# Merge gates as seven block products at the end of the first network, values of two groups there too, and square sums and scalings on ScalarE

## Chip, core and metric

The kernel runs on one core of one Trainium2 chip. The time is device microseconds of one execution; 2530.77 us is the median of 3 runs of the kernel before (2530.6 to 2532.81). A profile is one further execution, with its own time. PE is TensorE, DVE VectorE, ACT ScalarE, POOL GpSimd, SP the queue from which most transfers are issued.

## What is computed

One decoder layer on x of 1024 tokens x 1024 channels, all in float32:

```
x = x + 1/2 * SwiGLU_1(RMSNorm(x))
h = RMSNorm(x);  p = h @ w_in       # columns: q, k, v of 3 attention groups; q, k, v, beta,
                                    # decay and gate of 8 delta heads; merge gates g_a, g_b
A = dilated windowed attention, 3 groups x 4 heads of 64, softmax over the groups
B = gated delta rule, 8 heads of 128 (conv of 4 + silu, unit q and k, chunks), RMSNorm * silu(gate)
y = (sig(g_a) * (A @ w_branch_a) + sig(g_b) * (B @ w_branch_b)) @ w_out;   x = x + y
x = x + 1/2 * SwiGLU_2(RMSNorm(x));  out = RMSNorm(x)
```

g_a and g_b are 1024 x 1024 each: eight blocks of 128 columns of w_in for each, 16 in all.

## The kernel before

**Matmuls.** A float32 product is made of three float32r products: each operand v is split into H (v rounded, by an ACT copy) and L = v - H (by DVE), and xH wH + xL wH + xH wL is summed in PSUM. `ff_split` (L208 on, rows L216 and L217) splits a weight tile of 128x512, `split_to` (L166, L167) an activation. `proj` (L152 on, row L161) makes one 128-column block for one half of the 512 tokens with 8 k x 3 matmuls of 512 columns. Activations h are held transposed as `hH`, `hL`.

**First network** (`ff_hidden`, `ff_pair`, `ff_products`): the hidden blocks are made in pairs of columns. h (channels x tokens) and each weight pair are cut in 2x2 blocks, and seven block products (Winograd's form) stand in for eight: sums of blocks of h are made once (`ff_blocks`: T1, T2, T3, and a changed B12), the sums of the weight blocks per pair, and the products are accumulated or added in four PSUM banks (`QUAD_BANKS`) in the order `STEPS`. The first pairs use the order `FIRST`, which starts with products that need no sums (row L404). The down projection (`Down`, row L588) is a block form too. Its closing steps make h for the mixer (`make_h`), and then `First` multiplies h with the value columns of group 0 and the beta and decay columns (row L805), four token blocks before the last turns of h and four after, and stores them.

**Mixer** (`mixer`): three attention groups, each with its values (`values`: groups 1 and 2 as 16 token blocks x 24 matmuls of 256 columns, L701, evicted by ACT, stored and read back in another order), two pairs of heads with rotary q and k, and blocks of scores (L870), exp and products with V (L894). Then 8 delta heads. Per head: `gdn_keys` projects k and q, convolves them (L963 copy out of PSUM, L971 and L973 the four taps), transposes them (L983), squares and sums them per token (`ssq_tokens`: ACT square of 128x512 at L986, DVE reduction at L987), makes the decay matrix Dm (L1012 to L1015), and N and A as products of k and q with k (L1139) times a per-token factor and Dm (L1142, one DVE operation per chunk of 128). `gdn_inverse` sends blocks of N through DRAM, solves 32 rows on DVE (L1044 to L1050), sends them back, transposes (L1060) and merges the blocks with small matmuls (L1078 to L1100). `gdn_values` makes vb (L1164, L1165), `gdn_gate` the head's gate, `gdn_scan` runs over eight chunks one after the other (L1195 to L1219), squares and sums the output (L1226, L1227), scales it and transposes it (L1236).

**Merge gates** (`gate_tile`): one block of 128 columns is 2 x 24 matmuls into bank "mm", an ACT copy (L950) and a store for each half. `FILL` says how many are put where: two with the last attention pair, eight with the heads, the remaining six with the last head, together with `branch_a`. `merge_out` reads them back and multiplies.

**Order.** The program is traced once, `arrange` plans an order of the instructions for each engine from costs of its own (`Program.cost`) by the longest path to the end, and the kernel is built again with that order. It keeps the rings of tiles and of PSUM banks in the order of the program: "mm" has 2 banks, "ka" 9 tiles (k, q, kd, N and A of a head take five), "xp" 2, "vb", "g" and "Tm" 1. Tiles of a pool that is opened later wait for those of a closed one at the same place.

Of the kernel before, what the change touches and what calls it, by code (L numbers as in the profile page):

```python
# [8 lines left out]
F32 = mybir.dt.float32  # L9
# [275 lines left out]
    return res  # L285


def ff_blocks(C):


    nc = C.nc
    T1, T2, T3 = [[] for _ in range(3)]
    for i, T in ((2, T2), (1, T1), (3, T3)):
        for q in range(2):
            h, l = [C.fx.tile([P, 2, 512], F32R, name=f"t{i}{n}", tag="big", bufs=12) for n in "HL"]
            T += [(h[:, k], l[:, k]) for k in range(2)]
# [4 lines left out]
    keep = []

    def sums(ks):
        for k in ks:
            r = []
            for kk, ts in ((k, lo), (k, hi), (4 + k, lo), (4 + k, hi)):
                v = ff_e(C)
                nc.vector.tensor_tensor(out=v, in0=hH[:, kk, ts].bitcast(F32), in1=hL[:, kk, ts].bitcast(F32), op=ALU.add)
# [375 lines left out]
    return t[rows, (b - 1 if prev else b) * P:(b + 1) * P]  # L684


def values(C, I, w_in, g):

    nc = C.nc
    n = 256  # L690
    W = []
    with band(C, "bulk"):
        for k0 in (0, 4):
            halves = load_w(C, (lambda r: r[:, :4 * n].rearrange("p (k n) -> p k n", n=n),
                                cols(w_in, C_VA + g * 256, 256)[:, k0:k0 + 4, :]))
            W += [[v[:, i * n:i * n + n] for v in pair] for pair in halves for i in range(2)]
        for b in range(NT):
            ps = psum(C, "mm")
            for k in range(KT):
                for i, (h, w) in enumerate(((C.hH, 0), (C.hH, 1), (C.hL, 0))):  # L700
                    nc.tensor.matmul(ps[:, :n], h[:, k, b * P:b * P + P], W[k][w],  # L701
                                     start=k == 0 and i == 0, stop=k == KT - 1 and i == 2)
            v = C.at.tile([P, 256], F32, name="vs", tag="vs", bufs=2)
            nc.scalar.copy(v, ps[:, :256])
            nc.sync.dma_start(C.vd[g - 1][b * P:b * P + P, :], v)
# [77 lines left out]
class First:  # L783
# [193 lines left out]
def ssq_tokens(C, src, kd, out):  # L977

    nc = C.nc
    for q in range(2):  # L980
        ps = psum(C, "tA")
        for c in range(4):
            nc.tensor.transpose(ps[:, c * P:c * P + P], src[:, q * 4 + c, :], C.ident)  # L983
        v = ps.rearrange("p (c t) -> p c t", t=P)
        sq = C.gd.tile([P, 4, P], F32, name="sq", tag="sq", bufs=1)
        nc.scalar.activation(sq, v, AF.Square)  # L986
        nc.vector.tensor_reduce(out=out[:, q * 4:q * 4 + 4], in_=sq, axis=AX.X, op=ALU.add)  # L987
# [120 lines left out]
def gdn_keys(C, w_in, h, Dm):  # L1108
# [4 lines left out]
    with band(C, f"h{h}"):  # L1113
# [11 lines left out]
        ns = cl[:, 4]  # L1125
# [8 lines left out]
        for src, dst, sc in ((X.k, X.N, ns), (X.q, X.A, s)):  # L1134
            for q in range(2):
                ps = psum(C, "tA")
                for i in range(4):
                    c = q * 4 + i
                    nc.tensor.matmul(ps[:, i * P:i * P + P], X.k[:, c, :], src[:, c, :], start=True, stop=True)  # L1139
                for i in range(4):  # L1140
                    c = q * 4 + i
                    nc.vector.scalar_tensor_tensor(dst[:, c, :], ps[:, i * P:i * P + P], sc[:, c:c + 1], Dm[:, c, :],  # L1142
                                                   op0=ALU.mult, op1=ALU.mult)
# [10 lines left out]
def gdn_values(C, w_in, X):  # L1154
    nc = C.nc
    h = X.h
    with band(C, f"h{h}"):
# [3 lines left out]
        for q in range(2):  # L1161
            ps = psum(C, "tA")
            for c in range(4):
                nc.tensor.transpose(ps[:, c * P:c * P + P], vT[:, q * 4 + c, :], C.ident)  # L1164
            nc.vector.tensor_tensor(out=X.vb[:, q * 4:q * 4 + 4, :], in0=ps.rearrange("p (c t) -> p c t", t=P),  # L1165
                                    in1=X.nk[:, q * 4:q * 4 + 4].unsqueeze(2).to_broadcast([P, 4, P]), op=ALU.mult)
# [13 lines left out]
def gdn_scan(C, X):  # L1180
# [6 lines left out]
    with band(C, f"h{h}"):  # L1187
# [33 lines left out]
                S = Sn  # L1221

        so2 = C.gd.tile([P, 2, NT], F32, name="so2", tag="so2", bufs=2)
        for q in range(2):
            sq = C.gd.tile([P, 4, P], F32, name="sq", tag="sq", bufs=1)
            nc.scalar.activation(sq, o[:, q * 4:q * 4 + 4, :], AF.Square)  # L1226
# [683 lines left out]
```

## Times and profile before

| | |
|---|---|
| median of 3 runs | 2530.77 us |
| profiled execution, its own time | 2533.24 us |
| its span, first to last instruction | 2531.4 us |
| mean granted TensorE clock | 0.995 |
| network 1 up to its down projection | 0 to about 450 us |
| down projection and first values | about 450 to 703 us |
| attention | about 703 to 993 us |
| delta heads | about 980 to 1705 us |
| merge, norm and start of network 2 | about 1705 to 1931 us |
| network 2 | about 1931 to 2531 us |

Matmuls are pipelined, so that the busy time of one overlaps the next; the time of one in a stream is best read as a window's length over its count. A row of the groups names line, engine, operation, output<-inputs, shapes and count, then busy time, mean ns of one, and the engine's idle time before them with what ended it. A row of the table of windows gives each engine's busy time and count, the granted PE clock, the DMA share and GB/s. A row of a timeline or of the chain of waits gives start and length in us, then the engine and what it did.

### The profile page before, as it was taken

To read this page: it belongs to the slowest core of one execution; us is meant where nothing else is said; L and a number is where in the kernel's file an instruction comes from. 1 tells how busy PE (TensorE), PEld (TensorE's weight loads), DVE (VectorE), ACT (ScalarE), POOL (GpSimd) and SP (SyncE) were. 2 spreads that over 40 slices of the span, in tenths; PEclk is the share of its full clock that TensorE was granted. 3 is DMA by queue.
4 is the path that set the end of the run, shared out by engine and by line. 5 is a ranking of instruction groups with operands and counts; after the bars stand their busy time and mean duration, and the time that the engine had idled before them with its cause. 6 is when DMAs were issued, how large, how long until landed. Compare 5 with 4: busy or idle time off the path is not lost.

```text
span 2531.4 us, 34786 instructions
## 1 busy us (share of the span) xinstructions
PE 2488.5 (98%) x12739; PEld 2071.9 (82%) x12739; DVE 1766.7 (70%) x4035; ACT 983.8 (39%) x1881; POOL 26.5 (1%) x36
## 2 busy tenths in 40 slices
PE   7999999999999999999999999999999999999998
PEld 7888888888888888778777888888888888888886
DVE  7866666768734464878887888455768666667589
ACT  4432322444523346333454335254443332323444
POOL 0000000000000000000000000000000000000000
PEclk9999999999999999999999999999999999999999
DMA  4233224746343322222222223357532223238443
GB/s 163 84 109 117 92 104 175 269 125 205 122 124 94 100 78 64 61 53 55 78 65 64 55 75 84 105 200 286 199 126 83 100 92 121 90 118 305 137 163 133
DMA packets 259547, 308.39 MB, mean 122 GB/s; under 512 B 41680, under 2 KB 175024, under 8 KB 259376
## 3 DMA queue, kind: packets, MB, share of 16 engines
q1 hardware_dynamic: 257072, 299.88, 35.8%
q10 hardware_dynamic: 2304, 6.29, 1.1%
q8 instruction: 100, 1.64, 0.3%
q14 instruction: 71, 0.58, 0.1%
HBM read 221.01 MB, written 78.81 MB: 118 GB/s over the span
## 4 chain that ended last, share of the span: by engine, by line
PE 84%; DVE 11%; DMA 2%; ACT 1%; issue 1%; SPq 0%; DVEq 0%; ACTq 0%
PE mm L161 19%; PE tC L404 13%; PE mm L404 9%; PE tM L404 8%; PE mm L588 4%; PE tC L588 4%; PE tM L588 3%; PE tA L588 3%; PE tA L161 3%; PE mm L701 2%; PE mm L274 2%; PE tC L274 2%; DVE ka L973 2%; PE mm L1409 2%; PE tC L1409 1%; DVE fL L217 1%
## 5 line engine op out<-in xcount | busy, mean ns | idle before, releaser
L216 ACT CAST fH<-fraw 128x512 fp32r<-128x512 f32 x482 | 289.6, 620 | 603.4 <-PE tC L404 258.5
L217 DVE TENSOR_TENSOR fL<-fraw,fH 128x512 fp32r<-128x512 f32 x482 | 319.0, 685 | 161.5 <-ACT fH L216 147.0
L161 PE MATMUL mm<-hH,fH 128*128 128x512 f32 x896 | 360.3, 404 | 2.5 <-ACT xp L832 2.4
L161 PE MATMUL mm<-hL,fH 128*128 128x512 f32 x896 | 356.8, 399 | 0.0
L161 PE MATMUL mm<-hH,fL 128*128 128x512 f32 x896 | 353.9, 400 | 0.0
L161 PEld LDWEIGHTS mm<-hH,fH 128*128 128x128 f32 x896 | 170.1, 190 | 34.8 <-ACT xp L832 2.9
L161 PEld LDWEIGHTS mm<-hH,fL 128*128 128x128 f32 x896 | 169.6, 189 | 33.9 <-issue 1.0
L161 PEld LDWEIGHTS mm<-hL,fH 128*128 128x128 f32 x896 | 169.9, 190 | 30.5 <-issue 0.3
L404 PE MATMUL mm<-hH,fH 128*128 128x512 f32 x320 | 124.6, 389 | 0.0
L404 PE MATMUL mm<-hH,fL 128*128 128x512 f32 x320 | 123.7, 389 | 0.0
L404 PE MATMUL mm<-hL,fH 128*128 128x512 f32 x320 | 122.5, 389 | 0.0
L581 DVE TENSOR_TENSOR hid<-hid,fH 128x512 fp32r<-128x512 f32 x149 | 101.1, 684 | 10.1 <-ACT fH L580 10.1
L973 DVE SCALAR_TENSOR_TENSOR ka<-xp,cw,ka 128x512 f32<-128x512 f32 x96 | 74.9, 791 | 38.9 <-ACT ka L971 38.3
L580 ACT CAST fH<-hid 128x512 fp32r<-128x512 f32 x149 | 91.8, 616 | 14.6 <-PE tC L588 5.0
L216 ACT CAST fH<-hH 128x512 fp32r<-128x512 f32 x68 | 42.2, 622 | 84.7 <-PE tC L588 32.8
L431 DVE TENSOR_TENSOR e<-tC,e 128x512 f32<-128x512 f32 x40 | 27.3, 687 | 66.5 <-PE tC L404 66.5
L404 PEld LDWEIGHTS mm<-hH,fH 128*128 128x128 f32 x320 | 60.1, 188 | 12.7 <-ACT e L408 0.3
L404 PEld LDWEIGHTS mm<-hH,fL 128*128 128x128 f32 x320 | 60.1, 188 | 12.5
L588 PE MATMUL mm<-fH,hid 128*128 128x512 f32 x186 | 70.3, 389 | 0.0
L588 PE MATMUL tC<-fH,hid 128*128 128x512 f32 x186 | 70.3, 389 | 0.0
L404 PEld LDWEIGHTS mm<-hL,fH 128*128 128x128 f32 x320 | 60.1, 188 | 12.5
L351 DVE TENSOR_TENSOR s<-fraw 128x512 f32<-128x512 f32 x40 | 27.5, 687 | 54.0 <-DMA fraw<-in_ffn_w_gate_dram 53.4
(401 smaller groups left out, 6157.1 us busy)
## 6 DMA issues: line engine op xcount, KB each, us to landing
fraw<-in_w_in_dram SPq DMA_DIRECT2D x66, 512.0 KB, 3.8
fraw<-in_ffn_w_gate_dram SPq DMA_DIRECT2D x22, 1024.0 KB, 5.2
fraw<-in_ffn_w_up_dram SPq DMA_DIRECT2D x22, 1024.0 KB, 7.3
hL<-in_ffn_w_down_dram SPq DMA_DIRECT2D x8, 1024.0 KB, 6.6
fraw<-in_ffn_w_down_dram SPq DMA_DIRECT2D x8, 1024.0 KB, 5.9
fraw<-in_w_branch_b_dram SPq DMA_DIRECT2D x8, 1024.0 KB, 5.0
fraw<-in_w_out_dram SPq DMA_DIRECT2D x8, 1024.0 KB, 5.6
vb<-xp ACTq DMA_DIRECT2D x48, 128.0 KB, 2.4
```

What stands on the lines that cost most here:

```text
L161: nc.tensor.matmul(ps, w, x, start=k == 0 and i == 0, stop=k == kt - 1 and i == 2)
L216: nc.scalar.copy(h, src)
L217: nc.vector.tensor_tensor(out=l, in0=src, in1=h.bitcast(F32), op=ALU.subtract)
L274: nc.tensor.matmul(ps[:, n0:n0 + n], w, x[:, k, c], start=k == 0 and i == 0, stop=k == KT - 1 and i == 2)
L351: tt(out=s3[i], in0=a11, in1=a21, op=ALU.subtract)
L404: nc.tensor.matmul(ps, w, x, start=opens and k == 0 and q == 0, stop=k == 3 and q == 2, skip_group_check=True)
L580: C.nc.scalar.copy(h, v.bitcast(F32))
L581: C.nc.vector.tensor_tensor(out=v, in0=v.bitcast(F32), in1=h.bitcast(F32), op=ALU.subtract)
L588: self.C.nc.tensor.matmul(ps, x[:, m], w, start=p == 0 and i == 0, stop=p == NPAIR - 1 and i == 2)
L701: nc.tensor.matmul(ps[:, :n], h[:, k, b * P:b * P + P], W[k][w], start=k == 0 and i == 0, stop=k == KT - 1 and i == 2)
L973: nc.vector.scalar_tensor_tensor(o, x, w, o, op0=ALU.mult, op1=ALU.add)
L1409: nc.tensor.matmul(ps, mx[:, c], W[k][w], start=i == 0, stop=i == len(seq) - 1)
```

## The change

Fourteen of the sixteen gate blocks are made at the end of the first network, in seven pairs, with the seven block products; the last two stay with the last head. The block sums of h are made once more there, with the changed B12 in tiles of its own (`apart`), so that h stays as it is. The value products of groups 1 and 2 move there, between the first values and the pairs; their evicted tiles share the ring "s3" of 3 tiles, as those of the first values now do. In the heads, ACT sums the squares as it makes them, one chunk of 128 at a time, and scales Dm and vb per chunk; N and A are then made four chunks at a time. The planner adds 1000 ns to the expected end of each transfer.

```diff
-def ff_blocks(C):
+def ff_blocks(C, apart=False):
...
+    T4 = B12
+    if apart:
+        h, l = [C.fx.tile([P, 4, 512], F32R, name=n, tag=n, bufs=1) for n in ("vH", "vL")]
+        T4 = [(h[:, k], l[:, k]) for k in range(4)]
...
-            split_to(C, *B12[k], v)
+            split_to(C, *T4[k], v)
...
+def value_blocks(C, w_in, g):
...
+    for b in range(NT):
+        ps = psum(C, "tM")
...
+        v = ff_e(C, "vs", tag="s3")
+        nc.scalar.copy(v[:, :n], ps[:, :n])
+        nc.sync.dma_start(C.vd[g - 1][b * P:b * P + P, :], v[:, :n])
...
+GATES = [(C_GA + f * P, 0, f) for f in range(8)] + [(C_GB + f * P, 1, f) for f in range(8)]
+APART = 14
+def gate_pair(C, B, w_in, i, steps):
+    raw = ff_raw(C, cols(w_in, GATES[i][0], 256), 256)
...
+    def prepare(n):
+        if n == 6:
+            left[7] = ff_e(C, "s3", tag="s3").rearrange("p (k n) -> p k n", n=P)
+            tt(out=left[7], in0=a11, in1=a21, op=ALU.subtract)
+            tt(out=a21, in0=a21, in1=a22, op=ALU.add)
+            tt(out=a11, in0=a21, in1=a11, op=ALU.subtract)
+        elif n == 3:
+            tt(out=a12, in0=a12, in1=a11, op=ALU.subtract)
+        return ff_split(C, {1: a11, 6: a11, 5: a21, 2: a12, 4: a22, 3: a12, 7: left.get(7)}[n])
...
+    def run(chosen):
+        for n, b, opens in chosen:
...
+            for k in range(4):
+                xH, xL = B[n][k]
+                h, l = [v[:, k * P:k * P + P] for v in (H, L)]
+                for q, (x, w) in enumerate(((xH, h), (xL, h), (xH, l))):
+                    nc.tensor.matmul(ps, w, x, start=opens and k == 0 and q == 0, stop=k == 3 and q == 2,
+                                     skip_group_check=True)
...
+def gates_apart(C, w_in, between):
+    B, sums, last = ff_blocks(C, True)
+    sums(range(4))
+    between()
+    last()
+    for i in range(0, APART, 2):
+        steps = FIRST if i < 4 else STEPS
+        gate_pair(C, B, w_in, i, steps)(steps)
...
 def ssq_tokens(C, src, kd, out):
-        sq = C.gd.tile([P, 4, P], F32, name="sq", tag="sq", bufs=1)
-        nc.scalar.activation(sq, v, AF.Square)
-        nc.vector.tensor_reduce(out=out[:, q * 4:q * 4 + 4], in_=sq, axis=AX.X, op=ALU.add)
+        for c in range(4):
+            sq = C.gd.tile([P, P], F32, name="sq", tag="sq", bufs=2)
+            nc.scalar.activation(sq, v[:, c, :], AF.Square, accum_out=out[:, q * 4 + c:q * 4 + c + 1])
...
 def gdn_keys(C, w_in, h, Dm):
-        nc.vector.tensor_scalar(ns, s, -1.0, None, op0=ALU.mult)
+        for c in range(NT):
+            nc.scalar.activation(Dm[:, c, :], Dm[:, c, :], AF.Copy, scale=s[:, c:c + 1])
...
-                for i in range(4):
-                    c = q * 4 + i
-                    nc.vector.scalar_tensor_tensor(dst[:, c, :], ps[:, i * P:i * P + P], sc[:, c:c + 1], Dm[:, c, :],
-                                                   op0=ALU.mult, op1=ALU.mult)
+                nc.vector.scalar_tensor_tensor(dst[:, q * 4:q * 4 + 4, :], ps.rearrange("p (c t) -> p c t", t=P), sign,
+                                               Dm[:, q * 4:q * 4 + 4, :], op0=ALU.mult, op1=ALU.mult)
...
 def gdn_values(C, w_in, X):
-            nc.vector.tensor_tensor(out=X.vb[:, q * 4:q * 4 + 4, :], in0=ps.rearrange("p (c t) -> p c t", t=P),
-                                    in1=X.nk[:, q * 4:q * 4 + 4].unsqueeze(2).to_broadcast([P, 4, P]), op=ALU.mult)
+            for c in range(q * 4, q * 4 + 4):
+                nc.scalar.activation(X.vb[:, c, :], ps[:, (c - q * 4) * P:(c - q * 4) * P + P], AF.Copy, scale=X.nk[:, c:c + 1])
...
 def gdn_scan(C, X):
-        for q in range(2):
-            sq = C.gd.tile([P, 4, P], F32, name="sq", tag="sq", bufs=1)
-            nc.scalar.activation(sq, o[:, q * 4:q * 4 + 4, :], AF.Square)
-            nc.vector.tensor_reduce(out=so2[:, 0, q * 4:q * 4 + 4], in_=sq, axis=AX.X, op=ALU.add)
+        for c in range(NT):
+            sq = C.gd.tile([P, P], F32, name="sq", tag="sq", bufs=2)
+            nc.scalar.activation(sq, o[:, c, :], AF.Square, accum_out=so2[:, 0, c:c + 1])
...
-FILL = ((0, 0, 0, 0, 0, 2), (1, 1, 1, 1, 1, 1, 2))
+FILL = ((0, 0, 0, 0, 0, 0), (0, 0, 0, 0, 0, 0, 0))
...
-            first.blocks(range(4, NT))
+            def between():
+                first.blocks(range(4, NT))
+                for g in (1, 2):
+                    value_blocks(C, I["w_in"], g)
+            gates_apart(C, I["w_in"], between)
...
+MARGIN = 1000
...
             wire = end - tail
+            end += MARGIN
```

More of the change, by code (lines that the diff above doesn't have):

```diff
@@ L318, in sums @@
             keep.append(r21)
+    T4 = B12
+    if apart:
+        h, l = [C.fx.tile([P, 4, 512], F32R, name=n, tag=n, bufs=1) for n in ("vH", "vL")]
+        T4 = [(h[:, k], l[:, k]) for k in range(4)]
     def last():
         for k, v in enumerate(keep):
-            split_to(C, *B12[k], v)
-    return {1: B11, 2: B21, 3: B22, 4: B12, 5: T1, 6: T2, 7: T3}, sums, last
+            split_to(C, *T4[k], v)
+    return {1: B11, 2: B21, 3: B22, 4: T4, 5: T1, 6: T2, 7: T3}, sums, last
 FIRST = ((1, 0, True), (2, 0, False), (3, 3, True), (6, 1, True), (5, 2, True), (7, 1, False), (4, 1, False))
@@ L684, in seq_tokens @@
     return t[rows, (b - 1 if prev else b) * P:(b + 1) * P]
-def values(C, I, w_in, g):
+def value_blocks(C, w_in, g):
     nc = C.nc
@@ L691, in values @@
     W = []
-    with band(C, "bulk"):
[L693 to L705, printed above, removed]
+    for k0 in (0, 4):
+        halves = load_w(C, (lambda r: r[:, :4 * n].rearrange("p (k n) -> p k n", n=n),
+                            cols(w_in, C_VA + g * 256, 256)[:, k0:k0 + 4, :]))
+        W += [[v[:, i * n:i * n + n] for v in pair] for pair in halves for i in range(2)]
+    for b in range(NT):
+        ps = psum(C, "tM")
+        for k in range(KT):
+            for i, (h, w) in enumerate(((C.hH, 0), (C.hH, 1), (C.hL, 0))):
+                nc.tensor.matmul(ps[:, :n], h[:, k, b * P:b * P + P], W[k][w],
+                                 start=k == 0 and i == 0, stop=k == KT - 1 and i == 2)
+        v = ff_e(C, "vs", tag="s3")
+        nc.scalar.copy(v[:, :n], ps[:, :n])
+        nc.sync.dma_start(C.vd[g - 1][b * P:b * P + P, :], v[:, :n])
+def values(C, I, w_in, g):
+    nc = C.nc
+    with band(C, "bulk"):
         V = [None] * NT
@@ L821, in first_values, with keep @@
     return V
+GATES = [(C_GA + f * P, 0, f) for f in range(8)] + [(C_GB + f * P, 1, f) for f in range(8)]
+APART = 14
+def gate_pair(C, B, w_in, i, steps):
+    nc = C.nc
+    tt = nc.vector.tensor_tensor
+    raw = ff_raw(C, cols(w_in, GATES[i][0], 256), 256)
+    a11, a12, a21, a22 = [raw[:, q * 4:q * 4 + 4, m * P:m * P + P] for m in (0, 1) for q in (0, 1)]
+    early = steps is FIRST
+    banks = [None] * 4
+    left = {}
+    out = [(C.sgad, C.sgbd)[GATES[i + j][1]][GATES[i + j][2]] for j in (0, 1)]
+    def prepare(n):
[7 more added lines that the diff above has]
+        return ff_split(C, {1: a11, 6: a11, 5: a21, 2: a12, 4: a22, 3: a12, 7: left.get(7)}[n])
+    def keep(j, a, v):
+        nc.sync.dma_start(out[j][:, a * 512:a * 512 + 512], v)
+    weights = {}
+    for n in (1, 2, 6, 3, 5, 7, 4) if early else [n for n, _, _ in steps]:
+        weights[n] = prepare(n)
+    def run(chosen):
+        for n, b, opens in chosen:
+            if opens:
+                banks[b] = psum(C, QUAD_BANKS[b])
+            ps = banks[b]
+            H, L = weights[n]
+            for k in range(4):
[4 more added lines that the diff above has]
+                                     skip_group_check=True)
+            if n == 1:
+                run.p1 = ff_e(C)
+                nc.scalar.copy(run.p1, ps)
+            elif n == 6:
+                run.u2 = ff_e(C)
+                tt(out=run.u2, in0=ps, in1=run.p1, op=ALU.add)
+                if early:
+                    tt(out=run.u2, in0=banks[3], in1=run.u2, op=ALU.add)
+            elif n == 7:
+                u3 = ff_e(C)
+                tt(out=u3, in0=ps, in1=run.p1, op=ALU.add)
+                tt(out=u3, in0=banks[2], in1=u3, op=ALU.add)
+                keep(1, 1, u3)
+            elif n == 2:
+                c = ff_e(C)
+                nc.scalar.copy(c, ps)
+                keep(0, 0, c)
+            elif n == 4:
+                tt(out=run.p1, in0=ps, in1=run.p1, op=ALU.add)
+                keep(1, 0, run.p1)
+            elif n == (5 if early else 3):
+                tt(out=run.u2, in0=ps, in1=run.u2, op=ALU.add)
+                keep(0, 1, run.u2)
+    return run
@@ L1130, in gdn_keys @@
         nc.vector.tensor_scalar(X.so, rs[:, 8:16], float(P) ** -0.5, None, op0=ALU.mult)
-        nc.vector.tensor_scalar(ns, s, -1.0, None, op0=ALU.mult)
+        for c in range(NT):
+            nc.scalar.activation(Dm[:, c, :], Dm[:, c, :], AF.Copy, scale=s[:, c:c + 1])
         X.N, X.A = t4c(C, "ka"), t4c(C, "ka")
-        for src, dst, sc in ((X.k, X.N, ns), (X.q, X.A, s)):
+        for src, dst, sign in ((X.k, X.N, -1.0), (X.q, X.A, 1.0)):
             for q in range(2):
@@ L1309, in mixer @@
         C.bands[f"h{h}"] = base + 100000 + 20000 * h
-    gates = [(C_GA + f * P, C.sgad[f]) for f in range(8)] + [(C_GB + f * P, C.sgbd[f]) for f in range(8)]
+    gates = [(c, (C.sgad, C.sgbd)[i][f]) for c, i, f in GATES[APART:]]
     def fill(n):
```

3 lines of the change are left out of this document (1 added, 2 removed).

## The prediction

> **What bounds the kernel now.** I read the page's first lines, then the table of windows by stage, then the groups by form, and windows, chain and timeline of single stretches.
>
> ```profile
> span 2531.4 us, 34786 instructions
> PE 2488.5 (98%) x12739; PEld 2071.9 (82%) x12739; DVE 1766.7 (70%) x4035; ACT 983.8 (39%) x1881; POOL 26.5 (1%) x36
> PE 84%; DVE 11%; DMA 2%; ACT 1%; issue 1%; SPq 0%; DVEq 0%; ACTq 0%
> ```
>
> ```profile
> core 0: us, PE busy (x) PEld busy (x) DVE busy (x) ACT busy (x) POOL busy (x), PEclk, DMA share, GB/s
> 655.00:707.00 52.00, 52.00 (x348) 48.09 (x347) 30.11 (x83) 21.44 (x43) 0.00 (x0) 1.00 0.36 116
> 707.00:950.00 243.00, 240.55 (x1462) 205.01 (x1461) 121.39 (x301) 83.42 (x243) 1.92 (x2) 0.99 0.36 100
> 950.00:1075.00 125.00, 123.92 (x704) 100.82 (x705) 84.90 (x268) 62.93 (x135) 5.30 (x6) 1.00 0.22 61
> 1075.00:1705.00 630.00, 616.63 (x3689) 509.39 (x3688) 477.69 (x1444) 263.61 (x505) 19.06 (x24) 0.99 0.28 83
> 1935.00:2310.00 375.00, 375.00 (x1654) 310.07 (x1654) 250.99 (x407) 113.39 (x200) 0.00 (x0) 1.00 0.32 115
> ```
>
> The last row is the gate and up part of the second network, which works in the same seven-product form as the new gates: PE never pauses, and one 512-column matmul takes 375.00 / 1654 = 0.2267 us (the longer means of the groups below overlap). DVE is at 67% and ACT at 30% there. The mixer is different: from 1075 to 1705 PE loses 630.00 - 616.63 = 13.4 us, and DVE is at 76%. So PE sets the time nearly everywhere, work taken from PE is time as long as PE stays fed, and the place to look for losses is the mixer, where several chains of small steps are covered by projections. The gates are part of that cover.
>
> The profiled execution took 2533.24 us (span 2531.4), against a median of 2530.77 us; I work out differences on its rows and apply them to the median.
>
> **Gates as seven products.** One gate block is 2 halves x 8 k x 3 = 48 matmuls. Fourteen blocks are 672. Seven pairs of 7 products x 4 k x 3 = 84 are 588. That is 84 matmuls fewer, 84 x 0.2267 = 19.0 us. This is the only PE work that the change removes, and it is certain.
>
> What feeds the pairs:
>
> ```profile
> L217 DVE TENSOR_TENSOR fL<-fraw,fH 128x512 fp32r<-128x512 f32 x482 | 319.0, 685 | 161.5 <-ACT fH L216 147.0 <-PE tM L404 6.8 <-DMA U<-in_rope_dram 5.7
> L216 ACT CAST fH<-fraw 128x512 fp32r<-128x512 f32 x482 | 289.6, 620 | 603.4 <-PE tC L404 258.5 <-PE mm L161 81.8 <-DVE fraw L353 52.0
> L308 DVE TENSOR_TENSOR e<-hH,hL 128x512 f32<-128x512 f32 x32 | 20.2, 682 | 0.1
> 707.00:950.00 243.00, 48.67 (x384) 47.17 (x384) 0.99 0.36 100
> ```
>
> The last row is the window table for the value line L701 alone. A pair needs 3 sums, 7 splits and 5 evictions on DVE, 15 x 0.685 = 10.3 us, and 9 ACT operations, 9 x 0.62 = 5.6 us, beside 84 x 0.2267 = 19.0 us of PE. That is 54% of DVE and 29% of ACT, less than in the row 1935:2310 where PE doesn't pause: cost 0. Should feeding fail it would show at most at the first pair, whose 10 sums and splits are 7 us; that is the upper end. Its four stores and one load leave SP's queue in the mixer for this stretch, as the values' 16 stores and 4 loads do; PE waits for none of them there, since loads run two tiles ahead.
>
> The block sums of h are new: 4 x 11 + 4 = 48 DVE operations, 48 x 0.682 = 32.7 us, with 16 ACT splits, 9.9 us. Eight splits of the value weights come before, 8 x 0.685 = 5.5 us. The cover is the 384 value matmuls, 48.7 us, and four blocks of the first values: 38 us under about 60 us. Also, the first two pairs begin with products 1, 2 and 3, which need no sum. Cost 0; without the cover, up to 38 us.
>
> **Values moved.** The same 384 matmuls run earlier; their 48.7 us vanish from the attention stage and appear before it. Cost 0 as long as attention stays bound by PE: with 243 - 49 = 194 us left, DVE's 121 us are 63%. The evicted tile now has 3 buffers instead of 13 (first values) or 2: a block lasts 24 x 0.12 = 2.9 us, so three buffers are 8.7 us for a copy and a store. Nothing is queued behind it but the next copy.
>
> **Square sums and scalings by ACT.**
>
> ```profile
> L987 DVE TENSOR_REDUCE gssq<-sq 128x4 f32<-128x512 f32 x32 | 21.7, 679 | 4.4 <-ACT sq L986 4.1
> L986 ACT ACTIVATE sq<-tA 128x512 f32<-128x512 f32 x32 | 19.0, 594 | 9.6 <-DVE gssq L987 6.7 <-PE tA L983 1.3 <-PE tM L1100 1.1
> L1226 ACT ACTIVATE sq<-vb 128x512 f32<-128x512 f32 x16 | 10.1, 630 | 28.1 <-DVE vb L1219 28.1
> L1142 DVE SCALAR_TENSOR_TENSOR ka<-tA,cl,Dm 128x128 f32<-128x128 f32 x128 | 37.9, 343 | 0.4 <-issue 0.2
> L1165 DVE TENSOR_TENSOR vb<-tA,cl x16: 652/684/701, 1045.0 to 1619.1; 128x512 f32<-128x512 f32 x16
> L973 DVE SCALAR_TENSOR_TENSOR ka<-xp,cw,ka 128x512 f32<-128x512 f32 x96 | 74.9, 791 | 38.9 <-ACT ka L971 38.3
> L1201 ACT ACTIVATE qs<-tC,ex 128x128 f32<-128x128 f32 x56 | 20.5, 366 | 79.1 <-PE tC L1199 78.9
> L1205 ACT COPY v<-tC 128x128 f32<-128x128 f32 x64 | 16.9, 264 | 47.4 <-PE tC L1203 47.3
> L880 ACT ACTIVATION_READ_ACCUMULATOR s<-s,nm 128x1 f32 x96 | 18.0, 188 | 0.0
> ```
>
> DVE loses per head 6 reductions (4.1 us), 2 scalings of vb (1.4 us), and 16 small multiplies (37.9 / 8 = 4.7 us) that become 4 wide ones (4 x 0.79 = 3.2 us): 7.0 us. ACT gains per head 24 squares with a sum read out. No row has one alone; between a copy of that size (0.264) and a scaled one (0.366), plus the read-out of 0.188, it is 0.45 to 0.55 us, so 10.8 to 13.3 us. I take 10.8, since a square takes no scale from memory. Six wide squares go (4 x 0.594 + 2 x 0.630 = 3.6 us). The 16 scalings of Dm and vb are 16 x 0.366 = 5.9 us. Net ACT +13.1 us per head.
>
> One head's period, with the gates that go:
>
> ```profile
> 1237.00:1317.00 80.00, 78.41 (x485) 64.62 (x484) 66.99 (x202) 35.47 (x66) 3.32 (x4) 1.00 0.24 65
> 1237.00:1317.00 80.00, 62.41 (x241) 42.77 (x240) 1.00 0.24 65
> 993.00:1078.00 85.00, 83.36 (x482) 67.37 (x481) 69.36 (x196) 41.50 (x66) 4.71 (x5) 1.00 0.22 57
> 993.00:1078.00 85.00, 1.76 (x3) 1.00 0.22 57
> 1573.00:1705.00 132.00, 131.76 (x725) 109.22 (x724) 72.13 (x198) 51.57 (x103) 0.00 (x0) 1.00 0.44 146
> 1573.00:1705.00 132.00, 6.99 (x12) 1.00 0.44 146
> ```
>
> Of each two rows the first is all work, the second the projections (L161) or the gates' evictions alone. In 1237:1317 there are 241 projection matmuls, five blocks of 48: k, q, v, the head's gate and one merge gate. Without the merge gate 80 - 10.9 = 69.1 us of PE are left. DVE has 67.0 - 7.0 - 1.4 (the gate's splits) = 58.6 us, 85% of that, where it was 84%. ACT has 35.5 + 13.1 - 2.4 = 46.2 us, 67%. So the three engines shrink together, and I expect the period to follow PE with a little less ease: +0.5 us for each of seven heads, +3 us in all; between -5 (less DVE ahead of PE's small matmuls than now) and +25 (the rival below).
>
> The start of the heads (993 to 1078) is the stretch with least to spare. Three evictions are one and a half gates, 16.3 us of PE, so about 69 us of PE stay. DVE's 69.4 us lose the reductions, small multiplies and splits of nearly two heads, about 12 us, and much of the stretch is a chain over DVE. I take 73 us for it, a loss of 4 us; the ends are 0 and 16.3 us (nothing else moves up).
>
> The end of the heads (1573 to 1705) held twelve evictions, six gates; two stay. 132 - 4 x 10.9 = 88.4 us of PE are left for the last head's chain (two rows of DVE's timeline, then four of the chain of waits):
>
> ```profile
> 1577.40 0.17 DVE L1044 TENSOR_TENSOR fsP<-fsT,Tm 128x16 f32<-128x16 f32 x1
> 1608.54 1.24 DVE L1060 STREAM_TRANSPOSE Tm<-U 128x1024 f32<-128x1024 f32 x1
> ```
>
> ```profile
> 1648.68 0.62 PE tM L1078 x32
> 1657.66 0.60 PE tM L1100 x8
> 1660.54 0.22 PE tC L1203 x2
> 1702.31 0.87 PE tC L1236 x8
> ```
>
> From 1577.4 the inverse takes 32.4 us to 1609.8; then its merge waits 39 us for its turn on PE; merge, scan and closing transposes take 1703.2 - 1648.7 = 54.5 us. Without the wait this is 87 us from 1577.4, 91 us from 1573, against 88.4 us of PE: a loss of 2 us, between 0 and 10.
>
> The planner's margin makes it expect each transfer 1 us later. It adds no wait, but can reorder everything; transfers hold 2% of the chain of waits, so little hangs on when they are expected. I take 0, between -3 and +4.
>
> Sum: -19.0 + 3 + 4 + 2 = -10 us, from 2533.24 to 2523 for the profiled execution, from 2530.77 to **2521 us** for the median.
>
> **The rivals.**
>
> *The heads become a chain (slower).* Keys of head h+2 reuse tiles that the scan of head h frees:
>
> ```profile
> 1345.87 0.29 DVE L1219 TENSOR_TENSOR vb<-tC,qs 128x128 f32<-128x128 f32 x1 [1.31 <-PE tC L1215]
> 1346.73 0.57 ACT L963 COPY xp<-mm 128x512 f32<-128x512 f32 x1
> 1348.09 0.75 DVE L973 SCALAR_TENSOR_TENSOR ka<-xp,cw,ka 128x512 f32<-128x512 f32 x1
> ```
>
> The scan's last output at 1345.9 is followed at once by the next-but-one head's convolution. This loop spans two periods. It decides once it takes over 2 x 69.1 = 138 us, and the new ACT work in it (squares before the inverse, scalings of Dm) lengthens it by some 7 us. Today it lasts two periods, 2 x 80 = 160 us. If the two merge gates inside are all that leaves it, it is 160 - 21.8 + 7 = 145 us, 72.7 per period, and costs 7 x 3.6 = 25 us; with the 6 us of start and end, 2531 - 19 + 25 + 6 = 2543 us. For it speaks that it restarts without slack; against it, that in the last head waiting alone was 39 us, so the loop holds much that only waits for PE. Chance 0.15.
>
> *The saving is eaten at the edges (no change).* Start and end at their far ends cost 16 + 10 = 26 us; with a third of that regained by projections pulled forward, 17 us stay: 2531 - 19 + 17 = 2529 us. Chance 0.18.
>
> *PE pauses halve its clock (slower).*
>
> ```profile
> 1376.00:1380.00 4.00, 2.39 (x25) 2.00 (x23) 3.81 (x8) 2.80 (x6) 0.00 (x0) 0.76 0.01 4
> 1380.00:1384.00 4.00, 4.00 (x14) 3.33 (x13) 3.65 (x6) 2.26 (x5) 0.00 (x0) 0.50 0.17 66
> ```
>
> After 4 us in which PE worked 2.39, the next four ran at clock 0.50, 14 matmuls: about 2 us lost. If each of eight heads brings two such stretches more, 16 x 2 = 32 us go: 2531 - 19 + 32 = 2544 us. Chance 0.04, since the rows have few now. The Trainium skill ("TensorE: Matmul & The Clock Gate", "Part 1: The HAM clock gate (the "warmup" mystery)") speaks against taking cover from PE: after an idle window of about 3.4 us the clock is halved until PE has been busy for one. The trace agrees with the halving; that the whole window must be idle it doesn't show, since a stretch with PE busy for 2.39 of 4 us was enough.
>
> *All of it is kept.* Fewer switches and no loss at the edges: 2530.8 - 19 = 2512 us or some less. Chance 0.12. That the products are not fewer I rule out by the count.
>
> **How the numbers follow.** My forecast, 2514 to 2525.7, has the remaining 0.51. About 5 us (0.2%) is what a measurement here can tell from no change. Faster by more: 0.51 + 0.12 = 0.63. Within: 0.18. Slower: 0.15 + 0.04 = 0.19. The range goes from 2508 (all kept and 3 us of reordering) to 2541, which leaves out about half of the slower cases.
>
> **What would show it.** In the profile after: 84 matmuls fewer; a stretch of some 133 us before the mixer with PE at 100% and about 0.2267 us per matmul; heads about 70 us apart instead of 81; DVE near 85% and ACT near 67% there; PE's idle time in the mixer up by some 10 us. The forecast is wrong if heads follow each other at over 72 us, if PE pauses during the gate pairs, or if the granted clock drops in more than a few stretches.

## The result and the profile after

The change takes 2495.73 us (median of 4 runs, 2495.34 to 2496.77) against 2531.79 us before: a ratio of 0.9858 (95% interval 0.9843 to 0.9872), 36 us less. I had forecast 2521 us, and 2508 as the lowest. The direction was right; the gain is nearly twice what the count of products gives.

The page after, its span, busy line and chain by engine:

```profile
span 2495.0 us, 35187 instructions
PE 2457.7 (99%) x12655; PEld 2045.7 (82%) x12655; DVE 1787.9 (72%) x4001; ACT 1052.4 (42%) x2364; POOL 25.2 (1%) x36
PE 87%; DVE 7%; DMA 2%; ACT 2%; issue 1%; SPq 0%; ACTq 0%; DVEq 0%
```

PE has 12739 - 12655 = 84 matmuls fewer, as counted. For the rest, I cut both kernels at the same events: the first rotary copy out of PSUM, and the last closing transposes of the last head. First before, then after (there with the first network's end, and cut again at the last attention block and the first scan step); columns as in the prediction.

```profile
702.70:1703.20 1000.50, 983.61 (x5861) 817.33 (x5860) 682.19 (x2010) 409.27 (x882) 26.28 (x32) 0.99 0.30 85
```

```profile
695.00:741.00 46.00, 46.00 (x379) 45.78 (x378) 26.01 (x43) 14.00 (x30) 0.00 (x0) 1.00 0.13 44
741.00:885.20 144.20, 143.53 (x634) 118.28 (x632) 73.18 (x116) 39.17 (x71) 0.00 (x0) 1.00 0.32 104
885.20:1666.40 781.20, 770.49 (x4792) 633.13 (x4791) 595.70 (x1802) 421.94 (x1257) 24.95 (x32) 1.00 0.30 85
```

```profile
885.20:1107.30 222.10, 219.27 (x1249) 177.76 (x1248) 132.89 (x371) 93.03 (x288) 1.91 (x2) 1.00 0.38 103
1107.30:1185.70 78.40, 75.90 (x462) 62.32 (x461) 63.95 (x170) 47.94 (x143) 4.22 (x6) 1.00 0.22 56
1185.70:1666.40 480.70, 475.31 (x3084) 393.05 (x3083) 398.86 (x1263) 280.96 (x828) 18.82 (x24) 1.00 0.28 81
```

The mixer went from 1000.5 to 781.2 us. What left it by count is 672 x 0.2267 + 48.7 = 201.0 us, so it got 18.3 us shorter than that. The new stage ahead of it lasts 885.2 - 702.7 = 182.5 us, where 588 x 0.2267 + 48.7 = 182.0 was to be expected: the seven products and the values run at PE's pace from the start. After the mixer both kernels take the same, 2531.4 - 1703.2 = 828.2 and 2495.0 - 1666.4 = 828.6 us. So the question is the 18 us in the mixer. PE's idle time there fell from 1000.50 - 983.61 = 16.9 to 781.20 - 770.49 = 10.7 us, where I had expected it to rise. The rest is busy time: it fell by 213.1 us, 12 more than the 201.0 counted, and part of that is the granted clock, 0.99 before and 1.00 after.

### The profile page after: what moved, and what is told of

Its sections match the earlier page's. It is cut to its first block, busy times and chain, and to the rows that moved or that the text cites. A ratio compares the mean times of both kernels' runs of the same rounds, so it can differ in the third digit from the quotient of the medians.

```text
span 2495.0 us, 35187 instructions
## 1 busy us (share of the span) xinstructions
PE 2457.7 (99%) x12655; PEld 2045.7 (82%) x12655; DVE 1787.9 (72%) x4001; ACT 1052.4 (42%) x2364; POOL 25.2 (1%) x36
## 4 chain that ended last, share of the span: by engine, by line
PE 87%; DVE 7%; DMA 2%; ACT 2%; issue 1%; SPq 0%; ACTq 0%; DVEq 0%
PE mm L161 15%; PE tC L409 13%; PE mm L409 9%; PE tM L409 8%; PE mm L593 4%; PE tC L593 4%; PE tM L593 4%; PE tA L593 4%; PE tA L161 3%; PE tC L876 2%; PE tM L705 2%; PE mm L274 2%; PE tC L274 2%; PE mm L876 2%; PE mm L1498 2%; PE tC L1498 2%
## 5 line engine op out<-in xcount | busy, mean ns | idle before, releaser
L216 ACT CAST fH<-fraw 128x512 fp32r<-128x512 f32 x496 | 298.2, 621 | 634.2 <-PE tC L409 243.0
L217 DVE TENSOR_TENSOR fL<-fraw,fH 128x512 fp32r<-128x512 f32 x496 | 329.3, 687 | 108.5 <-ACT fH L216 90.3
L161 PE MATMUL mm<-hH,fH 128*128 128x512 f32 x672 | 272.2, 406 | 2.5 <-ACT xp L924 2.1
L161 PE MATMUL mm<-hL,fH 128*128 128x512 f32 x672 | 268.3, 400 | 0.0
L161 PE MATMUL mm<-hH,fL 128*128 128x512 f32 x672 | 263.1, 399 | 0.0
L161 PEld LDWEIGHTS mm<-hH,fH 128*128 128x128 f32 x672 | 126.9, 189 | 29.2 <-ACT xp L924 4.5
L161 PEld LDWEIGHTS mm<-hH,fL 128*128 128x128 f32 x672 | 126.8, 189 | 23.5 <-issue 0.3
L161 PEld LDWEIGHTS mm<-hL,fH 128*128 128x128 f32 x672 | 126.9, 189 | 21.2
L409 PE MATMUL mm<-hH,fH 128*128 128x512 f32 x320 | 124.5, 389 | 0.0
L409 PE MATMUL mm<-hH,fL 128*128 128x512 f32 x320 | 123.3, 389 | 0.0
L409 PE MATMUL mm<-hL,fH 128*128 128x512 f32 x320 | 122.5, 389 | 0.0
L409 PEld LDWEIGHTS mm<-hH,fL 128*128 128x128 f32 x320 | 60.1, 188 | 12.5
L409 PEld LDWEIGHTS mm<-hL,fH 128*128 128x128 f32 x320 | 60.1, 188 | 12.5
L409 PEld LDWEIGHTS mm<-hH,fH 128*128 128x128 f32 x320 | 60.0, 188 | 12.5
L216 ACT CAST fH<-hL 128x512 fp32r<-128x512 f32 x56 | 34.9, 623 | 71.4 <-PE tC L593 40.5
```

The costliest lines, as they stand in the source:

```text
L161: nc.tensor.matmul(ps, w, x, start=k == 0 and i == 0, stop=k == kt - 1 and i == 2)
L216: nc.scalar.copy(h, src)
L217: nc.vector.tensor_tensor(out=l, in0=src, in1=h.bitcast(F32), op=ALU.subtract)
L409: nc.tensor.matmul(ps, w, x, start=opens and k == 0 and q == 0, stop=k == 3 and q == 2, skip_group_check=True)
```

## The experiments

The change has three parts that can be undone alone: **place** (gates as products, values, and their new place), **ACT** (squares and scalings), and the planner's **margin**. Six kernels have every mix of them.

**Margin alone**, the kernel before with:

```diff
+MARGIN = 1000
...
             wire = end - tail
+            end += MARGIN
```

> The kernel before with the planner's margin of 1000 ns alone. The change took 36 us where the product count gives 19, so 17 us are to be explained. Theory M (the margin keeps planned work from standing behind transfers): 2531 - 17 = 2514 us. Theory D (relief of DVE by ACT) and theory L (the gates' and values' place): 2531 us, within 4 us.

2520.43 us, ratio 0.9953 (0.9939 to 0.9968): 12 us less. Of the three theories this speaks for the margin, though its 17 us aren't reached; two lines of the planner, which I had priced at 0, bring a third of the result on the old kernel.

**ACT alone**, the kernel before with the four edits of `ssq_tokens`, `gdn_keys`, `gdn_values` and `gdn_scan`:

```diff
-        nc.scalar.activation(sq, v, AF.Square)
-        nc.vector.tensor_reduce(out=out[:, q * 4:q * 4 + 4], in_=sq, axis=AX.X, op=ALU.add)
+        for c in range(4):
+            sq = C.gd.tile([P, P], F32, name="sq", tag="sq", bufs=2)
+            nc.scalar.activation(sq, v[:, c, :], AF.Square, accum_out=out[:, q * 4 + c:q * 4 + c + 1])
```

> The kernel before with the square sums and scalings on ACT alone. Theory D (DVE is what PE's small matmuls wait for in the heads, and the waits halve the clock): up to 17 us less, 2514 us. Theories M and L: 2531 us, within 4 us; the chain rival of the prediction would have it slower.

2530.02 us, ratio 0.9989 (0.9979 to 0.9998): about 2 us. Relief of DVE is not the source of the 17.

**Place alone**, the kernel before with the rest of the diff:

```diff
-FILL = ((0, 0, 0, 0, 0, 2), (1, 1, 1, 1, 1, 1, 2))
+FILL = ((0, 0, 0, 0, 0, 0), (0, 0, 0, 0, 0, 0, 0))
...
+            gates_apart(C, I["w_in"], between)
```

> The kernel before with the seven-product gates and the moved values alone, squares and scalings on DVE, no margin. All theories have the 19 us of the product count. Theory L: 2496 us. Theories M and D: 2512 us; if DVE becomes the bound of the shorter head period (67 of 70 us), slower than that, 2520 us or more.

2523.18 us, ratio 0.9971 (0.9961 to 0.9981). Only 9 of the 19 us of the count arrive: theory L falls, and some 10 us are lost again. That DVE has become the bound, which I had at 2520 us or more, would fit this number too; the kernel with the margin and without ACT's part (below) speaks against it.

**Plain products at the new place.** The kernel after, but each of the fourteen blocks with 48 matmuls:

```diff
-    B, sums, last = ff_blocks(C, True)
-    sums(range(4))
     between()
-    last()
-    for i in range(0, APART, 2):
-        steps = FIRST if i < 4 else STEPS
-        gate_pair(C, B, w_in, i, steps)(steps)
+    for i in range(APART):
+        c0, j, f = GATES[i]
+        W = load_w2(C, cols(w_in, c0))
+        for a in (0, 1):
+            pg = proj(C, W, a, QUAD_BANKS[i % 2 * 2 + a])
+            m = ff_e(C)
+            C.nc.scalar.copy(m, pg)
+            C.nc.sync.dma_start((C.sgad, C.sgbd)[j][f][:, a * 512:a * 512 + 512], m)
```

> The kernel after with the fourteen gate blocks at their new place, made by plain products (48 matmuls each, no block sums). The count alone: 84 matmuls x 0.2267 us more than after, 2496 + 19 = 2515 us. If the block form costs something that is hidden in the result (sums, first pair), less than 19 us more.

2517.59 us, 21.9 us more than after. The product count's 19.0 us stand, with 3 us on top. Cut at the same events, the stage ahead of the mixer lasts 200.7 us (702.7 to 903.4) against 182.5: 18.2 us of difference, so the sums and evictions of the block form cost under 1 us. The 3 us on top lie in attention, 225.8 against 222.1 us.

**Pairs of parts.** The kernel after without ACT's part, which undoes the four edits shown above with the wide squares, the scaled evictions and the scaled decays that belong to them:

```diff
-            sq = C.gd.tile([P, P], F32, name="sq", tag="sq", bufs=2)
-            nc.scalar.activation(sq, v[:, c, :], AF.Square, accum_out=out[:, q * 4 + c:q * 4 + c + 1])
+        sq = C.gd.tile([P, 4, P], F32, name="sq", tag="sq", bufs=1)
+        nc.scalar.activation(sq, v, AF.Square)
+        nc.vector.tensor_reduce(out=out[:, q * 4:q * 4 + 4], in_=sq, axis=AX.X, op=ALU.add)
...
-            nc.scalar.activation(Dm[:, c, :], Dm[:, c, :], AF.Copy, scale=s[:, c:c + 1])
+        nc.vector.tensor_scalar(ns, s, -1.0, None, op0=ALU.mult)
```

> The kernel after with squares and scalings back on DVE (place and margin stay). Place alone was 2523, margin alone -12. If the parts simply add: 2523 - 12 = 2511 us, and ACT's part with the rest in place is 15 us although it was 2 us alone, because DVE binds only once the heads lose their gates. If the margin also cures what place alone lost: about 2500 us, and ACT's part is 4 us.

Without the margin:

```diff
-MARGIN = 1000
...
-            end += MARGIN
```

> The kernel after without the planner's margin. If the margin acts on its own, as alone: 2496 + 12 = 2508 us. If it only mended stalls that the gates' cover made, nothing: 2496 us.

And without the place: the gates are plain products among the heads and the values lie among the attention blocks, as in the kernel before.

```diff
-FILL = ((0, 0, 0, 0, 0, 0), (0, 0, 0, 0, 0, 0, 0))
+FILL = ((0, 0, 0, 0, 0, 2), (1, 1, 1, 1, 1, 1, 2))
...
-            gates_apart(C, I["w_in"], between)
```

> The kernel before with margin and ACT's part, gates and values where they were. If both act on their own: 2532 - 12 - 2 = 2518 us. Then place brings 22 us on top of them, 19 by the count and 3 by fewer switches.

| place | ACT | margin | us |
|---|---|---|---|
| | | | 2531.8 to 2532.9 |
| | | x | 2520.43 |
| | x | | 2530.02 |
| x | | | 2523.18 |
| | x | x | 2527.34 (ratio 0.9978, 0.9969 to 0.9987) |
| x | | x | 2497.55 (0.9862, 0.9846 to 0.9879) |
| x | x | | 2517.93 (0.9943, 0.9928 to 0.9957) |
| x | x | x | 2495.73 (0.9858, 0.9843 to 0.9872) |

The first of the three came out as its second branch had it (about 2500 us). The other two missed: without the margin I had 2508 or 2496 us, and without the place 2518, 9 us too low. The parts don't add. With the place, the margin is worth 2523.2 - 2497.6 = 26 us without ACT's part and 22 us with it, twice what it is on the old kernel; at the old place with ACT's part it is worth only 2530.0 - 2527.3 = 3 us. With the margin, the place is worth 2520.4 - 2497.6 = 23 us without ACT's part: the 19.0 of the count and 4 more. ACT's part is worth 2 us at most in the kernel after, which these runs can't tell from nothing; with the margin and the gates among the heads it costs 7 us.

Where the 22 us are shows in the kernel without the margin, cut at the same three events as above:

```profile
887.00:1120.20 233.20, 223.67 (x1248) 181.36 (x1247) 133.53 (x371) 93.30 (x287) 1.92 (x2) 0.98 0.37 97
1120.20:1194.80 74.60, 71.09 (x438) 58.23 (x436) 63.10 (x169) 47.48 (x140) 4.34 (x6) 1.00 0.24 62
1194.80:1686.20 491.40, 482.51 (x3109) 396.75 (x3108) 398.28 (x1264) 286.28 (x833) 18.91 (x24) 1.00 0.28 79
```

Its mixer lasts 799.2 us, and 1000.5 - 201.0 = 799.5: without the margin the mixer shrinks by what was taken out, no more and no less. The margin takes 11.1 us from attention. The heads' two stretches have to be read together, since 24 matmuls lie in the first of them after and in the second without the margin: 74.6 + 491.4 = 566.0 against 78.4 + 480.7 = 559.1 us, 6.9 us. That is 18.0 us in all. PE's idle time is 21.9 us against 10.7. The other 6.8 us are busy time for the same 4795 matmuls; in attention the granted clock is 0.98 against 1.00. What PE waited for in attention (window 900 to 1100), without the margin and then after:

```profile
PE tA L986 <- DVE pT L981: 3.4, 2, 3.0
PE tC L962 <- DVE ka L931: 2.7, 1, 2.7
PE tC L962 <- DVE o L966: 1.7, 3, 1.1
```

```profile
PE mm L161 <- ACT xp L924: 1.6, 2, 1.4
PE tM L979 <- ACT s L972: 0.3, 1, 0.3
PE tA L986 <- DVE pT L981: 0.2, 1, 0.2
```

The longest of these waits can be followed to its source. Two rows of DVE's timeline without the margin, the row of PE that waited, and two windows:

```profile
1018.72 1.23 DVE L928 TENSOR_TENSOR xp<-xp,U 128x1024 f32<-128x1024 f32 x1 [6.04 <-DMA vb<-xp]
1022.57 1.01 DVE L981 COPY pT<-tM 128x256 f32<-128x256 f32 x2
1023.04 2.31 PE L986 MATMUL tA<-ka,pT 128*128 128x64 f32 x12 [2.97 <-DVE pT L981]
```

```profile
1020.00:1024.00 4.00, 1.03 (x8) 0.89 (x8) 4.00 (x6) 0.00 (x0) 0.00 (x0) 0.99 0.00 0
1024.00:1028.00 4.00, 4.00 (x18) 3.70 (x18) 2.28 (x4) 0.37 (x1) 0.00 (x0) 0.58 0.33 84
```

`vb<-xp` are the swaps of the rotary halves, small transfers from one tile to another; without the margin they land 2.2 to 8.2 us after their issue, with a median of 2.9. When the planner believes that one lands early, it puts the multiplication that needs it (L928) ahead of other work in DVE's order. Here DVE stood 6.04 us for it. The transposes that PE had made for the copies of L981 ended at 1018.45, but those copies stood behind the rotary work until 1022.57; PE waited 2.97 us for them, and its clock fell to 0.58 in the next window.

A long wait alone doesn't show a loss. DVE's longest wait for a swap is at the first rotary tile, without the margin (first) and after (second):

```profile
898.28 1.23 DVE L928 TENSOR_TENSOR xp<-xp,U 128x1024 f32<-128x1024 f32 x1 [9.68 <-DMA vb<-xp]
```

```profile
896.38 1.22 DVE L928 TENSOR_TENSOR xp<-xp,U 128x1024 f32<-128x1024 f32 x1 [5.55 <-DMA vb<-xp]
```

In both kernels the multiplication starts 11.2 to 11.3 us after the first rotary copy (887.0 and 885.2). Over the whole execution DVE's waits for swaps add up to nearly the same, 27.8 us without the margin and 26.4 after; what differs is which work stands behind them.

In the heads the matter is less clear. DVE's waits from 1000 to 1690 for the swaps and for the inverse's transfers (`nbd`, `ud`), without the margin:

```profile
DVE xp L928 <- DMA vb<-xp: 9.9, 2, 6.0
DVE Tm L1123 <- DMA Tm<-nbd: 2.8, 3, 1.7
DVE Tm L1152 <- DMA U<-ud: 2.7, 4, 1.1
DVE vT L1065 <- DMA Tm<-nbd: 1.4, 3, 0.7
DVE S L1303 <- DMA Tm<-nbd: 1.2, 1, 1.2
```

After, no wait for the inverse's transfers is left, and of the swaps' this one:

```profile
DVE xp L928 <- DMA vb<-xp: 10.7, 4, 2.9
```

But the kernel with place and margin and without ACT's part, which is as fast within 2 us, still has waits of 2.8 us for `nbd` and 3.3 us for `ud`. So that these short waits are the heads' 6.9 us is not shown. Splitting the margin says more.

**Margin for the swaps alone, and for all but the swaps** (q is 2 for ACT's queue, which issues only these):

```diff
-            end += MARGIN
+            if q == 2:
+                end += MARGIN
```

> The kernel after with the margin for the swaps of the rotary halves alone (the transfers issued by ACT, 48 of them). Without any margin it was 2518, with all of it 2496. In the traces some 13 of those 22 us were lost before the last attention block. If the swaps' late landings (planned early, with blocks of scores behind them) are that part: 2505 us. If it is all of it: 2496. If the swaps don't matter: 2518.

> The kernel after with the margin for all transfers but the swaps of the rotary halves. The complement of the run before: 2509 us if the swaps are 13 us of it, 2518 if all hangs on them, 2496 if they don't matter.

2510.31 us (0.9914, 0.9899 to 0.9929) and, with `q != 2`, 2503.61 us (0.9888, 0.9873 to 0.9903): 7.6 and 14.3 us less than without any, 21.9 together against 22.2 for both at once. The two add, and act in different places. The swaps' margin first, then the rest's, cut at the same events (the heads' start between the two rows is left out):

```profile
884.80:1110.20 225.40, 219.21 (x1245) 178.03 (x1245) 132.32 (x372) 91.92 (x284) 1.91 (x2) 1.00 0.39 101
1184.20:1680.30 496.10, 487.04 (x3108) 400.42 (x3108) 398.24 (x1264) 286.71 (x833) 19.83 (x24) 0.99 0.28 79
```

```profile
885.70:1115.90 230.20, 222.19 (x1248) 180.40 (x1247) 133.84 (x371) 94.62 (x289) 1.92 (x2) 0.99 0.37 98
1195.30:1674.00 478.70, 473.79 (x3084) 391.37 (x3083) 398.48 (x1263) 280.92 (x828) 19.17 (x24) 1.00 0.28 81
```

The swaps' margin mends attention (233.2 to 225.4 us) and leaves the heads long: with their start, 74.0 + 496.1 = 570.1 us against 566.0 without any margin. The rest's takes 3.0 us from attention (230.2) and 7.9 from the heads (79.4 + 478.7 = 558.1). The rest holds the inverse's transfers, but also all loads and stores; which of them it is in the heads was not tried and stays open.

**More margin**, to tell late landings from a fortunate order:

```diff
-MARGIN = 1000
+MARGIN = 2000
```

> The kernel after with a margin of 2000 ns. If transfers still land later than planned: a few us less, 2490. If 1000 covers what they are late by: 2496 within 4. If being planned late costs something of its own: more than 2500.

> The kernel after with a margin of 500 ns; 0 ns is 2518, 1000 is 2496, 2000 is 2504. Late landings: between, about 2507. Chance of the order: anywhere from 2496 to 2518, without relation to its neighbours.

> The kernel after with a margin of 800 ns. Late landings: 2496 to 2502. Chance of the order: as likely above 2504 as below.

> The kernel after with a margin of 1200 ns. Late landings: 2494 to 2499. Chance of the order: as likely above 2504 as below.

> The kernel after with a margin of 1500 ns. Late landings: 2494 to 2502, between its neighbours. Chance of the order: as likely above 2504 as below.

> The kernel after with a margin of 900 ns. Steady fall: 2496 to 2499. If 1000 is a fortunate single order: 2500 to 2506.

> The kernel after with a margin of 1100 ns. If there is a step from some value on: either near 2496 or near 2504. If 1000 is a fortunate single order: 2500 to 2506, like its neighbours.

| margin, ns | 0 | 500 | 800 | 900 | 1000 | 1100 | 1200 | 1500 | 2000 |
|---|---|---|---|---|---|---|---|---|---|
| us | 2517.9 | 2507.0 | 2498.9 | 2495.4 | 2495.7 | 2500.5 | 2504.8 | 2506.3 | 2503.6 |
| attention, profiled | 233.2 | 228.5 | 226.2 | 221.4 | 222.1 | 226.4 | 227.1 | 231.3 | 225.1 |
| heads with their start, profiled | 566.0 | 562.6 | 556.7 | 559.0 | 559.1 | 556.9 | 561.2 | 564.1 | 564.4 |

The last two rows are cut at the same events as above. The time falls steadily up to 900 or 1000 ns, rises by 9 us up to 1200, and stays there. The theory of late landings has the fall right within 1 us at 500, 800 and 900 ns, and misses at 1200 and 1500, where it had 2494 to 2499 and 2494 to 2502 us. Any margin tried from 500 ns on is some 11 us or more better than none, so the gain hangs on no single order. But attention is 4 to 5 us lower at 900 and 1000 ns than at 800 and 1100, while the heads are no longer at those two than at 900 and 1000: some 4 us of the 22 may be a fortunate order of the attention blocks. That planning transfers too late costs something of its own is one reading of the rise; no run separates the two.

**Values back among the attention blocks**, as in the kernel before:

```diff
...
                 first.blocks(range(4, NT))
-                for g in (1, 2):
-                    value_blocks(C, I["w_in"], g)
```

> The kernel after with the value products of groups 1 and 2 back among the attention blocks; the first values alone cover the block sums. The moved values cost PE nothing by the prediction: 2496 us within 4, if 33 us of sums on DVE stay covered by products 1 to 3 and the first values. Without that cover up to 20 us more.

2504.81 us (0.9893, 0.9878 to 0.9907), 9 us more than after. PE's longest wait of this run at that place, and two windows there:

```profile
PE tC L891 <- ACT fH L216: 9.1, 1, 9.1
```

```profile
690.00:700.00 10.00, 6.61 (x43) 5.79 (x42) 10.00 (x17) 3.09 (x6) 0.00 (x0) 1.00 0.08 28
700.00:710.00 10.00, 3.81 (x8) 2.60 (x9) 10.00 (x18) 5.49 (x10) 0.00 (x0) 0.54 0.00 0
```

DVE is busy for all 20 us with the block sums, PE for 10.4, and its clock falls to 0.54. The moved values are the sums' cover, as the prediction named it. The price at the place is higher than 9 us: the stage lasts 148.9 us (702.7 to 851.6) where 588 x 0.2267 = 133.3 are due, 15.6 us lost, of which 5 come back in the heads (553.8 us with their start, against 559.1).

**All sixteen blocks in pairs**, so that the last head keeps no gate:

```diff
-APART = 14
+APART = 16
```

> The kernel after with all sixteen gate blocks in eight pairs, so that the last head keeps only the branch of attention as cover. The count gives 12 x 0.2267 = 2.7 us less: 2493 us. By the prediction's working of the last head (chain 91 us, PE 88.4 with two gates) PE has 66.6 us left for a chain of about 85: some 18 us lost, 2511 us.

2504.33 us (0.9892, 0.9877 to 0.9907): 9 us slower, not 15, although PE has 12 matmuls fewer. Its window at the last head, and then the same window after:

```profile
1610.00:1630.00 20.00, 15.11 (x70) 11.55 (x70) 19.64 (x68) 11.72 (x29) 0.00 (x0) 0.91 0.47 144
```

```profile
1610.00:1630.00 20.00, 19.93 (x156) 15.34 (x154) 10.95 (x18) 10.21 (x24) 0.00 (x0) 1.00 0.74 245
```

PE stands for 4.9 of 20 us there, and its clock drops; with two gates left it stands for 0.1. Cut at the same events, the mixer takes 775.5 us, 5.7 less than after, though two blocks or 96 x 0.2267 = 21.8 us left it: 16 us are lost, near the 18 I had. Behind the mixer 7.6 us come back (821.0 us against 828.6), which I had not foreseen.

## Why the prediction was wrong

**Right: 84 matmuls, 19.0 us.** Measured 21.9 us against plain products at the same place, 18.2 us of it in the stage itself. The pairs ran at 133.37 / 583 = 0.229 us per matmul, near the 0.2267 forecast; this is the window table after for the pairs' line alone:

```profile
741.00:885.20 144.20, 133.37 (x583) 109.24 (x583) 1.00 0.32 104
```

**Right: block sums, pairs and values at 0, with their cover named.** Taking the cover away cost 9 us, 15.6 at the place, within the "up to 38".

**Near in sum by luck, for the kernel without margin: the mixer's losses.** I added 3 + 4 + 2 us for heads, start and end. Without the margin the mixer lost 0 (799.2 against 799.5 us). The whole was 2517.9 us where my sum said 2521, because some 4 us went elsewhere, where I had put nothing: 2.3 in the stage ahead of the mixer (702.7 to 887.0 is 184.3, against 182.0) and 1.4 behind it (829.6 against 828.2).

**The step that failed is the margin: "I take 0, between -3 and +4".** It is 22 us in this kernel, and of the 25 us between my 2521 and the result nearly all. The reason I gave, that transfers hold 2% of the chain of waits, doesn't hold: after the change they hold 2% as well. The chain shows what ended last. Where DVE stood 6.04 us for a swap with copies queued behind it, PE's own wait was for DVE, 2.97 us, and a slower clock came on top. The margin for the swaps alone takes 7.8 of attention's 11.1 us; in the heads the stretch is known (6.9 us) and the transfer isn't. A hint stood in the trace before, in the list of who waited for whom, and I did not price it:

```profile
DVE xp L836 <- DMA vb<-xp: 19.9, 7, 4.6
DVE Tm L1060 <- DMA U<-ud: 13.2, 3, 9.0
```

With the margin alone, on the old kernel, the first of these is 11.9 us in 3 waits, and the second is gone.

**The rivals.** The slower chain of heads did not come: the heads' stretch is 480.7 us from the first scan on. Three windows after, each from one head's first row of the inverse to the next one's:

```profile
1250.50:1318.50 68.00, 67.40 (x440) 55.43 (x439) 60.37 (x185) 40.80 (x122) 3.03 (x4) 1.00 0.24 63
1318.50:1383.40 64.90, 64.03 (x423) 53.37 (x423) 57.05 (x178) 39.81 (x120) 2.76 (x4) 1.00 0.25 64
1383.40:1451.10 67.70, 67.45 (x437) 55.52 (x436) 57.41 (x180) 40.28 (x120) 3.62 (x4) 1.00 0.24 61
```

The period is 66.9 us, below my 69.6, with DVE at 87% and ACT at 60%. So the loop over two heads can be shorter than 138 us. That what I called its lack of slack was work waiting for PE is the likely reading; no run tries it. Stretches at a halved clock became fewer, not more (mean 0.995 before, 0.998 after).

**Mis-sized: ACT's part.** I worked out 7 us of DVE per head and had the three engines shrink together by it. Without it the kernel takes 2497.6 against 2495.7 us: the heads with their start take 562.7 us against 559.1, with DVE at 89% instead of 83%. ACT's price was too high: I added the times of a square and its read-out, which overlap. The 24 squares of a head take 7.9 us of ACT (below) where I took 10.8, and its 16 scalings 2.45 + 2.34 = 4.8 us where I took 5.9; so ACT is at 60% and not 67%. A smaller slip: a matmul of 256 columns takes 48.67 / 384 = 0.127 us, not 0.12. Neither moves the sum.

## What to carry to other kernels

When the order of instructions is planned ahead, the expected landing of transfers is a parameter with a price: an engine that takes its instructions in order stops for a late transfer with all that is behind it, as DVE did above. So plan landings on the late side, and sweep by how much; the best value here held for two neighbours only. Read the list of who waited for transfers also where the engine isn't the bound, and don't judge it by the chain of waits. Its totals are no price either: look for a wait behind which the engine that sets the time then stood. Filler work is cover: before it is moved or shortened, find what runs beside it, and keep as much as the last uncovered chain needs.

## What the runs showed of the hardware

A square of 128x128 on ACT with its sum read out, in the kernel after:

```profile
L1079 ACT ACTIVATE sq<-tA x128: 258/286/373, 1111.3 to 1564.7; 128x128 f32<-128x128 f32 x128
L1079 ACT ACTIVATION_READ_ACCUMULATOR sq<-tA x128: 192/219/307, 1111.4 to 1564.8; 128x1 f32 x128
```

The two can't be added. Three rows of ACT's timeline, and ACT's busy time in one head's window for the squares of k and q (16 squares, 32 records) and for those of the scan's output (8 squares):

```profile
1111.27 0.26 ACT L1079 ACTIVATE sq<-tA 128x128 f32<-128x128 f32 x1
1111.42 0.19 ACT L1079 ACTIVATION_READ_ACCUMULATOR sq<-tA 128x1 f32 x1
1111.52 0.27 ACT L1079 ACTIVATE sq<-tA 128x128 f32<-128x128 f32 x1
```

```profile
1250.50:1318.50 68.00, 4.65 (x32) 1.00 0.24 63
1250.50:1318.50 68.00, 3.23 (x16) 1.00 0.24 63
```

The read-out starts before the square's record ends, and the next square before the read-out's: squares in a row start every 0.25 us. Sixteen of them take 4.65 us, 0.29 each, where 4 wide squares took 2.4 us of ACT and 4 reductions 2.7 us of DVE. Squares that stand alone, in the scan, take 0.40 us.

The clock halves without a wholly idle window. In the kernel with ACT's part and the margin at the old place, whose mean clock was 0.993:

```profile
1280.00:1284.00 4.00, 3.11 (x75) 2.18 (x72) 3.91 (x8) 3.98 (x13) 0.00 (x0) 1.00 0.02 4
1284.00:1288.00 4.00, 3.39 (x17) 2.22 (x18) 3.84 (x7) 3.06 (x7) 1.41 (x2) 0.65 0.81 234
1288.00:1292.00 4.00, 4.00 (x17) 3.04 (x17) 3.79 (x9) 2.82 (x16) 0.00 (x0) 0.50 0.01 3
```

PE was busy for 3.11 of 4 us with small matmuls, its longest pause there was 0.76 us, and the clock fell in the next window. The Trainium skill ("TensorE: Matmul & The Clock Gate", "Part 1: The HAM clock gate (the "warmup" mystery)") gives an idle window of about 3.4 us as the condition in its table of the two states. This trace doesn't agree: a window of many small matmuls, transposes among them, and short pauses was enough. Which of these it takes is not shown.
